# A two-layer diffusion block: modulation by bursts on TensorE, and the remaining row steps in one chain through the up and down passes

## The chip, the cores and the metric

The kernel runs on one core of a Trainium2 chip. The metric is the time of one execution on the device in microseconds (us), given as the median over several runs. A core has engines that run side by side and wait for each other by semaphores: TensorE (PE, matrix multiplications, with its weight loads PEld), VectorE (DVE, elementwise work and reductions), ScalarE (ACT), GpSimd (POOL) and SyncE (SP, which here issues nearly all DMA transfers). Each engine works through its own instructions in a fixed order.

## The reference

Two layers over 1024 latent tokens and 256 context tokens of width 1024. In each layer half of the heads are a bidirectional mLSTM and half a two-dimensional neighbourhood attention; an output projection and a squared-ReLU MLP (1024 to 4096 to 1024) follow. Six modulation vectors of 1024 values (shift, scale and gate for either half of the layer) come from the conditioning vector `c` for the latent tokens and from `c_ctx` for the context:

```python
for l in range(DEPTH):
    need_ctx = l < DEPTH - 1
    mod = silu_c @ w_ada[l] + b_ada[l]          # 1024 -> 6 * 1024
    mod_c = silu_cc @ w_ada[l] + b_ada[l]
    sh1, sc1, g1, sh2, sc2, g2 = split(mod, 6)  # and sh1c ... from mod_c
    h = rmsnorm(x, norm1_g[l]) * (1.0 + sc1) + sh1
    hc = rmsnorm(xc, norm1_g[l]) * (1.0 + sc1c) + sh1c
    y, yc = token_mixers(h @ w_in[l], hc @ w_in[l], ...)   # mLSTM and attention
    x = x + g1 * (y @ w_out[l])
    h = rmsnorm(x, norm2_g[l]) * (1.0 + sc2) + sh2
    x = x + g2 * sq_relu_mlp(h, w_mlp1[l], w_mlp2[l])
    if need_ctx:
        ...                                     # the same for xc with sh1c ... g2c
return rmsnorm(x, final_g)
```

The change is about how `mod` and `mod_c` are computed, a product of two vectors with a 1024 x 6144 matrix per layer, and about where in the program that happens.

## The kernel before

All matrix products are in float32 precision by splitting each operand into a high and a low part and adding three products; the three matmuls of `mm3` are lines L85, L86 and L87, and the splitting of weights is at L80 and L926. The 6144 columns of the modulation are counted as 12 blocks of 512: blocks 0 to 3 are shift and scale of the first half, 4 and 5 the gate `g1`, 6 to 9 shift and scale of the second half, 10 and 11 the gate `g2`.

The first layer's stages in time: an opening to some 70 us, in which blocks 0 to 3 are made; keys, values and gates of the mLSTM to 132 us; the mLSTM output in 20 tiles (`mlstm_out`, `mlstm_tile`) to 449; the neighbourhood attention (`na`, 4 pairs of heads with 2 context blocks and 8 blocks of latent rows each, 40 in all) to 723; the output projection to 840; the up pass of the MLP (`up`) to 1197; the passage to the down pass; the down pass (`down`) to 1505, and a context part to 1625. The second layer follows with the same stages, without context outputs (its attention has 32 blocks) and without any modulation work, since its vectors are made in the first layer.

There are two ways to compute modulation. `ada` does it on TensorE: for each of eight contraction blocks of 128, one matmul per block of 512 columns, with the two silu vectors as 32 stationary columns (L144), each block in its own 32-column tile of the array and its own 32 partitions of one PSUM bank; then a copy of the bank by VectorE (L154), four transposes (L157) and additions of the bias. `ada_rows` does it on VectorE: for each group of 128 output values and each of the two vectors it loads 512 KB of the transposed matrix (L178, tile `wada`, one buffer, with the silu vector as its second half from L175), and one custom instruction multiplies by the silu row and sums (L183, followed by a read of the accumulator). The text calls this a row step. Blocks 4 and 5 are 16 row steps (two vectors), blocks 6 to 9 are 32.

Both are generators. Other code calls `next` on them, so that one piece is issued at a time between other work; the order of each engine is the order in which the code issues. In the first layer's mixers `self.fill` is a chain of row steps for blocks 4 to 9, 48 in all. `tick` takes one piece; it is called at the end of `project_j` (a projection inside the mLSTM output) and after every block of the attention, and whatever is left is issued after the third pair. In `up`, a second chain makes blocks 10 and 11 and the second layer's blocks 0 to 3 (48 steps), three per round with the rest at the last round but one; a third one makes the second layer's blocks 4 to 11 for one vector (32 steps) from round n = 7 of `down` on, every second round, and in the context part.

Other lines that the text names: L475, L495, L601, L611, L612, L624 and L654 are small matmuls and transposes of an mLSTM tile, L493 and L642 DVE work of it; in the attention L823 and L833 are scores, L828 and L834 the maxima on DVE, L839 and L840 the reciprocal and the scaling of the softmax, L848, L859 and L867 transposes, L860 and L868 the copies of them, L874 the product with the values, and L721, L706 and L760 evictions of query, key and output; at the passage L1056 and L1050 store hidden values, L1193 and L1241 load weights and hidden values of the down pass, L1399 loads x, L925 and L926 split what was loaded.

Of the kernel before, what the change touches and what calls it, by code (L numbers as in the profile page):

```python
# [10 lines left out]
F32 = mybir.dt.float32  # L11
# [35 lines left out]
class Kern:  # L47
    def __init__(self, tc, d):
        self.tc, self.nc, self.d = tc, tc.nc, d
        self.fill = iter(())  # L50
# [7 lines left out]
    def tick(self):  # L58

        next(self.fill, None)  # L60
# [72 lines left out]
    def ada(self, l, blocks, tag, pool, bufs):  # L133

        nc, d, ws, nb = self.nc, self.d, [], len(blocks)
# [4 lines left out]
        for k in range(KT + bufs):  # L140
            if k >= bufs:
                w = ws.pop(0)
                for j in range(nb):
                    nc.tensor.matmul(acc[32 * j:32 * j + 32, :], self.silu[:, k - bufs, :], w[:, j, :], start=k == bufs, stop=k - bufs == KT - 1,  # L144
                                     skip_group_check=True, tile_position=(0, 32 * j))
            if k < KT:
                w = pool.tile([128, nb, 512], F32, name="wada", bufs=bufs)
                src = d["w_ada"][l, k * 128:(k + 1) * 128, :].rearrange("p (b c) -> p b c", c=512)
                nc.sync.dma_start(w[:], src[:, blocks[0]:blocks[-1] + 1:blocks[1] - blocks[0], :])
                ws.append(w)  # L150
            yield
        m = 32 * nb
        rv = pool.tile([128, 512], F32, name="arow")
        nc.vector.tensor_copy(rv[:m, :], acc[:m, :])  # L154
        tp = self.bank(tag)
        for t in range(4):
            nc.tensor.transpose(tp[:, t * m:(t + 1) * m], rv[:m, t * 128:(t + 1) * 128], self.ident[:m, :m])  # L157
        for j, b in enumerate(blocks):
            src = tp[:, :4 * m].rearrange("p (t c) -> p t c", t=4)[:, :, 32 * j:32 * j + 2]
            fs = slice(4 * b, 4 * b + 4)  # L160
            nc.vector.tensor_add(mod[:, fs, :], src, self.bada[l][:, fs].unsqueeze(2).to_broadcast([128, 4, 2]))
            for v in range(2):
                self.gain(l, b, v)
        yield

    def ada_rows(self, l, blocks, vectors):
# [5 lines left out]
        t = self.cp.tile([128, 2, D], F32, name="wada")  # L172
        raw, row = t[:, 0], t[:, 1]
# [202 lines left out]
    def project2(self, W, i, hi, lo, tag="mm"):  # L376
        acc = self.bank(tag)
        for u in range(2):
            for k in range(KT):
                wh, wl = W[k // 4]  # L380
                ws = slice((k % 4) * 256, (k % 4) * 256 + 256)
                self.mm3(acc[:, u * 256:(u + 1) * 256], self.toktile(hi[k], 2 * i + u), self.toktile(lo[k], 2 * i + u), wh[:, ws], wl[:, ws], k == 0, k == KT - 1)
        return acc[:].rearrange("p (u c) -> p u c", u=2)

    def project_g(self, W, i, hi, lo, tag="mm", accs=None, ks=range(KT), us=range(2)):

        accs = accs or [self.bank(tag) for _ in range(2)]
        for u in us:
            acc = accs[u]
            for k in ks:  # L390
                wh, wl = W[k // 3]
                ws = slice((k % 3) * 288, (k % 3) * 288 + 288)
                self.mm3(acc[:, :288], self.toktile(hi[k], 2 * i + u), self.toktile(lo[k], 2 * i + u), wh[:, ws], wl[:, ws], k == 0, k == KT - 1)
        return accs

    def project_j(self, W, i, hi, lo, cols):
# [9 lines left out]
        self.tick()  # L406
# [161 lines left out]
    def mlstm_tile(self, l, pr, i, acc):  # L568
# [35 lines left out]
        yield  # L604
        hh = mp.tile([128, 2, 2, 2, 65], F32, name="hh", bufs=1)
# [186 lines left out]
    def na(self, l, hi, lo, need_ctx, Wq, accs, last):  # L792

        self.wide = 1
# [188 lines left out]
    def up(self, l, ctx, B, hi, lo, hp_, hid, filler, last):  # L983
# [155 lines left out]
        def run(pool):  # L1139
            rest_.append(pool)  # L1140
            for j in range(NP):
# [30 lines left out]
    def down(self, l, hid, we, alloc):  # L1172
# [113 lines left out]
        def run(x, mod, load, after, filler):  # L1286
# [3 lines left out]
            for n, (p, b, s) in enumerate(whole):  # L1290
# [10 lines left out]
                if n > 6 and n % 2:  # L1301
                    next(filler, None)
# [236 lines left out]
    def run(self):  # L1539
        nc, d = self.nc, self.d  # L1540
        PS = bass.MemoryType.PSUM
        with self.open(name="pad", side="right") as pad, self.open(name="const") as self.cp, self.open(name="w") as self.wp, \
# [17 lines left out]
            for l in range(DEPTH):  # L1560
# [5 lines left out]
                ada = [chain(self.ada_rows(l, range(10, 12), range(2)), self.ada_rows(l + 1, range(4), range(2))), self.ada_rows(l + 1, range(4, 12), range(1))] if need_ctx else [iter(())] * 2  # L1566
# [16 lines left out]
                with self.open(name=f"x{l + 1}", side="right") as xp, self.open(name=f"up{l}") as hp_, contextlib.ExitStack() as right:  # L1583
# [6 lines left out]
                    prep, lead, rest = self.up(l, need_ctx, B, hi, lo, hp_, hid, ada[0], start)  # L1590
# [53 lines left out]
                with self.open(name=f"xd{l}") as xp, self.open(name=f"sd{l}") as self.sp, self.open(name=f"we{l}") as wx:  # L1644
# [7 lines left out]
                    if l == DEPTH - 1:  # L1652
                        finish(x, mod, load, lambda *a: self.final(x, *a), ada[1])
# [24 lines left out]
                    finish(x, mod, load, after, ada[1])  # L1678
                    run_all(ada[1])
# [150 lines left out]
```

## Time and profile before

| | us |
|---|---|
| median of 3 runs | 2924.03 |
| lowest and highest | 2919.05 and 2924.76 |
| the profiled execution | 2928.78 |
| its span, first to last instruction | 2927.0 |

The mean granted clock of TensorE was 0.991 of full speed in the profiled execution. All durations below are from that execution. In the rows that follow, a group line gives line, engine, operation, tiles (out<-in), shapes and count, then busy us and the mean ns of one, then the idle time ahead of it and what ended it. A line of waits names engine, bank and line that waited, what it waited for, the total us, how often, and the longest. A line of the timeline gives start, duration and, in brackets, the idle time before it. In a line of the chain of work stand start, duration and what the time was spent on. After the change the line numbers are larger by some 5 to 22.

### The profile page before, as it was taken

Reading aid. Unit: us, or ns where it says so; the run is one execution under the profiler, and the core shown is the slowest. Engines: PE = TensorE matmul, PEld = TensorE weight load, DVE = VectorE, ACT = ScalarE, POOL = GpSimd, SP = SyncE. Lnnn points to the kernel's source line nnn. Section 1 sums busy time; section 2 is a strip of 40 time slices with the busy share of each in tenths; the row PEclk is TensorE's granted clock in tenths of the full one; section 3 lists DMA queues with packets and bytes.
Section 4 is the critical chain, followed back from the end, with each engine's and each line's share of the span. In section 5 each row is a group of like instructions: output and inputs, shape, how many; then the busy total and the mean of one; then the engine's idle time right before and its main releaser. Section 6 shows DMA issues by size and latency. Waiting matters only on the chain.

```text
span 2927.0 us, 45550 instructions
## 1 busy us (share of the span) xinstructions
PE 2849.7 (97%) x16512; PEld 2413.8 (82%) x16512; DVE 2252.4 (77%) x5156; ACT 1267.3 (43%) x2426; POOL 67.3 (2%) x117
## 2 busy tenths in 40 slices
PE   7999999998999999999999999999999999999998
PEld 4888888777888888878889988888888788888888
DVE  6789987886598777779878678877875987768774
ACT  5333334454463333344445323335564633334453
POOL 0000000001000000000000000000010000000000
PEclk9999999998999999999999999999999999999999
DMA  7323333555637555797977122213356354469673
GB/s 244 105 94 111 102 99 122 170 186 166 195 113 250 194 191 198 236 366 267 334 266 272 61 87 66 68 62 110 97 154 214 118 183 155 158 233 314 209 254 105
DMA packets 275394, 506.85 MB, mean 173 GB/s; under 512 B 23616, under 2 KB 111680, under 8 KB 275168
## 3 DMA queue, kind: packets, MB, share of 16 engines
q1 hardware_dynamic: 275168, 503.93, 52.2%
q8 instruction: 130, 2.13, 0.3%
q14 instruction: 96, 0.79, 0.1%
HBM read 408.25 MB, written 95.59 MB: 172 GB/s over the span
## 4 chain that ended last, share of the span: by engine, by line
PE 56%; DMA 5%; DVE 5%; ACT 2%; issue 1%; SPq 1%; POOL 0%; DVEq 0%; ACTq 0%; POOLq 0%
PE q L87 11%; PE q L86 11%; PE q L85 11%; PE mm L85 6%; PE mm L86 6%; PE mm L87 6%; PE q L874 1%; PE q L624 1%; DMA wraw<-yscr 1%; DMA wraw<-w_out 1%; DMA raw<-w 1%; DMA wraw<-hid 1%; PE q L848 1%; DVE wlo L80 1%; PE q L833 1%
## 5 line engine op out<-in xcount | busy, mean ns | idle before, releaser
L85 PE MATMUL q<-ah,whi 128*128 128x512 f32 (+1 forms) x1488 | 555.9, 374 | 7.8 <-ACT ah L925 7.3
L86 PE MATMUL q<-al,whi 128*128 128x512 f32 (+1 forms) x1488 | 555.2, 373 | 0.1
L87 PE MATMUL q<-ah,wlo 128*128 128x512 f32 (+1 forms) x1488 | 554.0, 372 | 1.0 <-DVE wlo L926 0.9
L85 PE MATMUL mm<-ah,whi 128*128 128x512 f32 (+1 forms) x1104 | 381.8, 346 | 7.0 <-DVE nq L721 6.2
L87 PE MATMUL mm<-ah,wlo 128*128 128x512 f32 (+1 forms) x1104 | 380.5, 345 | 0.0
L86 PE MATMUL mm<-al,whi 128*128 128x512 f32 (+1 forms) x1104 | 380.4, 345 | 0.0
L85 PEld LDWEIGHTS q<-ah,whi 128*128 128x128 f32 x1488 | 280.8, 189 | 57.9 <-ACT ah L925 8.2
L87 PEld LDWEIGHTS q<-ah,wlo 128*128 128x128 f32 x1488 | 280.8, 189 | 51.4 <-DVE wlo L926 1.8
L86 PEld LDWEIGHTS q<-al,whi 128*128 128x128 f32 x1488 | 281.0, 189 | 50.4 <-issue 1.7
L85 PE MATMUL mm<-whi,ah 128*128 128x512 f32 (+2 forms) x864 | 315.3, 365 | 1.0 <-DVE st L294 0.9
L86 PE MATMUL mm<-wlo,ah 128*128 128x512 f32 (+2 forms) x864 | 311.0, 360 | 0.0
L87 PE MATMUL mm<-whi,al 128*128 128x512 f32 (+2 forms) x864 | 309.6, 358 | 0.0
L85 PEld LDWEIGHTS mm<-ah,whi 128*128 128x128 f32 x1104 | 209.6, 190 | 33.3 <-DVE nq L721 6.8
L87 PEld LDWEIGHTS mm<-ah,wlo 128*128 128x128 f32 x1104 | 209.7, 190 | 25.5 <-issue 0.7
L86 PEld LDWEIGHTS mm<-al,whi 128*128 128x128 f32 x1104 | 209.8, 190 | 24.4 <-issue 0.2
L925 ACT CAST ah<-raw 128x512 fp32r<-128x512 f32 (+1 forms) x264 | 144.1, 566 | 141.5 <-PE q L87 69.3
L85 PEld LDWEIGHTS mm<-whi,ah 128*128 128x128 f32 x864 | 164.6, 191 | 25.4 <-PE q L475 1.3
L87 PEld LDWEIGHTS mm<-whi,al 128*128 128x128 f32 x864 | 164.8, 191 | 23.2 <-issue 0.5
L86 PEld LDWEIGHTS mm<-wlo,ah 128*128 128x128 f32 x864 | 165.0, 191 | 22.0 <-issue 0.5
L926 DVE TENSOR_TENSOR al<-raw,ah 128x512 fp32r<-128x512 f32 (+1 forms) x264 | 158.1, 620 | 27.7 <-ACT ah L925 27.5
L183 DVE CUSTOM_DVE_ANT_0 wada<-wada,consts 128x1024 f32<-128x1024 f32 x128 | 163.3, 1276 | 19.9 <-DMA wada<-w_adaT 19.6
L926 DVE TENSOR_TENSOR wlo<-raw,whi 128x1024 fp32r<-128x1024 f32 x84 | 102.4, 1222 | 77.3 <-ACT whi L925 74.9
(278 smaller groups left out, 5292.0 us busy)
## 6 DMA issues: line engine op xcount, KB each, us to landing
raw<-w SPq DMA_DIRECT2D x168, 512.0 KB
wada<-w_adaT SPq DMA_DIRECT2D x128, 512.0 KB
raw<-hid SPq DMA_DIRECT2D x104, 512.0 KB
wraw<-w SPq DMA_DIRECT2D x80, 512.0 KB
hid<-hb SPq DMA_DIRECT2D x128, 256.0 KB
hid<-ht SPq DMA_DIRECT2D x96, 256.0 KB
gb<-gscr SPq DMA_DIRECT2D x36, 512.0 KB
wraw<-w_j SPq DMA_DIRECT2D x32, 512.0 KB
```

The costliest lines, as they stand in the source:

```text
L80: nc.vector.tensor_sub(lo[:, :n], raw[:, :n], fview(hi[:, :n]))
L85: mm(out, lh, rh, start=start, stop=False, skip_group_check=True)
L86: mm(out, lh, rl, start=False, stop=False, skip_group_check=True)
L87: mm(out, ll, rh, start=False, stop=stop, skip_group_check=True)
L183: nc.vector.tensor_tensor_reduce(raw, raw, row, 1.0, self.bada[l][:, i:i + 1], ALU.mult, ALU.add, mod[:, i, v:v + 1])
L624: nc.tensor.matmul(n4[:, s, h, :], P[:, s, h, :], va[:, u, h, :], start=True, stop=True, skip_group_check=True)
L833: mm(sl[:, :nl].rearrange("p (r w) -> p r w", w=Rw[1]), q[2 * h + z], krhs[h], start=z == 0, stop=z == 1)
L848: nc.tensor.transpose(tp[:, (h * 2 + a) * 128:(h * 2 + a + 1) * 128], Pn[h][:, a * 128:(a + 1) * 128], self.ident)
L874: mm(yp[h * 64:(h + 1) * 64, :], v[h], pt[h], start=i == 0, stop=i == len(tiles) - 1, skip_group_check=True)
L925: ins = self.nc.scalar.copy(hi, src)
L926: self.nc.vector.tensor_sub(lo, src, fview(hi))
```

## The change

Blocks 6 to 9 of the first layer move from row steps to `ada` on TensorE. `ada` gets a second form for `bufs=1`: four blocks share one tile of weights, so a column slice is 256 instead of 512 wide, two contraction blocks are loaded together (two DMAs of 512 KB), and one burst of eight matmuls (L150) works through them. Two column slices of four such bursts make eight bursts. The pieces are taken at more places: `project2` and `project_g`, which belong to keys, values and gates, as well as `project_j` and each `mlstm_tile`. Blocks 4 and 5 stay row steps, but in a second generator, `self.rows`, of which `tick(True)` takes a piece only when `fill` is used up. The attention no longer ticks; `na` issues what is left of both at its start. In `up` and `down`, one chain holds all 80 row steps: three per round of `up` to the fourteenth round and one in the last two, then every second round of `down` from n = 3 on, and then in the context part.

```diff
-    def tick(self):
-
-        next(self.fill, None)
+    def tick(self, rows=False):
+
+        if next(self.fill, self) is self and rows:
+            next(self.rows, None)
...
-    def ada(self, l, blocks, tag, pool, bufs):
+    def ada(self, l, blocks, tag, pool=None, bufs=1):
...
+        n = 1024 // nb
+        todo = [(k, o) for o in range(0, 512, n) for k in range(KT)]
+        two = 2 if bufs == 1 else 1
+        def through(k, o, w):
+            for z in range(two):
                 for j in range(nb):
-                    nc.tensor.matmul(acc[32 * j:32 * j + 32, :], self.silu[:, k - bufs, :], w[:, j, :], ...)
+                    nc.tensor.matmul(acc[32 * j:32 * j + 32, o:o + n], self.silu[:, k + z, :], w[:, z, j, :], ...)
+        for i in range(0, len(todo) + bufs * two, two):
+            if i >= bufs * two:
+                through(*todo[i - bufs * two], ws.pop(0))
+            if i < len(todo):
+                k, o = todo[i]
+                w = pool.tile([128, two, nb, n], F32, name="wada", bufs=bufs)
+                for z in range(two):
+                    src = d["w_ada"][l, (k + z) * 128:(k + z + 1) * 128, :].rearrange("p (b c) -> p b c", c=512)
+                    nc.sync.dma_start(w[:, z], src[:, blocks[0]:blocks[-1] + 1:blocks[1] - blocks[0], o:o + n])
+                    if z < two - 1:
+                        yield
                 ws.append(w)
             yield
...
     def project2, project_g (at their ends)
+        self.tick()
...
     def project_j
-        self.tick()
+        self.tick(True)
...
     def mlstm_tile (after the copy of qT)
+        self.tick(i in (2, 4))
...
     def na
+        run_all(self.fill)
+        run_all(self.rows)
...
-                self.tick()
             run_all(nxt)
-            if pr == 2:
-                run_all(self.fill)
...
     def up
-                for _ in range(2):
+                for _ in range(2 if j < NP - 2 else 0):
                     next(filler, None)
-                if j == NP - 2:
-                    run_all(filler)
...
     def down
-                if n > 6 and n % 2:
+                if n > 2 and n % 2:
                     next(filler, None)
...
     def mixers
-            self.fill = chain(*(self.ada_rows(l, blocks, range(2)) for blocks in (range(4, 6), range(6, 10))))
+            self.fill = self.ada(l, range(6, 10), "q")
+            self.rows = self.ada_rows(l, range(4, 6), range(2))
...
-                ada = [chain(self.ada_rows(l, range(10, 12), range(2)), self.ada_rows(l + 1, range(4), range(2))), self.ada_rows(l + 1, range(4, 12), range(1))] if need_ctx else [iter(())] * 2
+                ada = chain(*(self.ada_rows(*a) for a in ((l, range(10, 12), range(2)), (l + 1, range(4), range(2)), (l + 1, range(4, 12), range(1))) if need_ctx))
```

What this does to the order of the engines is shown at three places. The first is PE in one of the mLSTM output tiles; `mm<-whi,ah` are the projections' matmuls, `q<-kva,P` the product with the values. Before:

```order
L624 MATMUL q<-kva,P 128x65 x8
L85 MATMUL mm<-whi,ah_89 128x512
L86 MATMUL mm<-wlo,ah_89 128x512
L87 MATMUL mm<-whi,al_113 128x512
L85 MATMUL mm<-whi,ah_92 128x512
L86 MATMUL mm<-wlo,ah_92 128x512
```

Now:

```order
L646 MATMUL q<-kva,P 128x65 x8
L150 MATMUL q<-wada,silu 32x256 x8
L86 MATMUL mm<-whi,ah_89 128x512
L87 MATMUL mm<-wlo,ah_89 128x512
L88 MATMUL mm<-whi,al_113 128x512
L86 MATMUL mm<-whi,ah_92 128x512
```

A burst of eight matmuls stands behind the product with the values and ahead of the next projection; the fourth to the eighth burst lie so, one in each of five tiles.

The second place is DVE in the attention's first pair. `nq` and `nk1` are the query and key evictions, `S` the scores of a block, `smax` and `ssum` their maximum and sum. Before:

```order
L721 TENSOR_TENSOR nq_5133<-mm_5102,nq_5133 64x512
L721 TENSOR_TENSOR nq_5134<-mm_5102,nq_5133 64x512
L706 SCALAR_TENSOR_TENSOR nk1_5160<-mm_5169,nk1_5160 64x256
L183 ISA wada_4396,mod_179<-wada_4396,consts_153 128x1024
L183 ISA mod_179 128x1
L839 RECIPROCAL ssum_5208<-ssum_5208 128x1
L828 ISA S_5212,smax_5213<-q_5200,zero_159 128x256
```

Now:

```order
L743 TENSOR_TENSOR nq_5231<-mm_5200,nq_5231 64x512
L743 TENSOR_TENSOR nq_5232<-mm_5200,nq_5231 64x512
L728 SCALAR_TENSOR_TENSOR nk1_5258<-mm_5267,nk1_5258 64x256
L860 RECIPROCAL ssum_5304<-ssum_5304 128x1
L849 ISA S_5308,smax_5309<-q_5296,zero_159 128x256
```

The row step between the evictions and the softmax of the next block is gone, as are all 30 in this stage; the rest of DVE's order is as it was.

The third place is SP at the passage from up to down, from the first load of hidden values to the loads of x (`hid` and `hidc0` are stores of hidden values, `wraw<-w2` and `raw<-w2` the down weights). Before:

```order
L178 DMA wada_10647<-w_adaT 128x1024
L1193 DMA wraw_12727<-w2 128x2x512
L178 DMA wada_10647<-w_adaT 128x1024
L1056 DMA hid0_81<-hb_12683 128x512
L1241 DMA wraw_12733<-hid0_81 128x2x512
L1056 DMA hid0_81<-ht_12719 128x512
L1193 DMA wraw_12791<-w2 128x2x512
L178 DMA wada_10647<-w_adaT 128x1024
L1056 DMA hid0_81<-hb_12716 128x512
```

Now:

```order
L1212 DMA wraw_12747<-w2 128x2x512
L1077 DMA hid0_81<-hb_12701 128x512
L1260 DMA wraw_12753<-hid0_81 128x2x512
L196 DMA wada_10680<-w_adaT 128x1024
L1077 DMA hid0_81<-ht_12739 128x512
L1077 DMA hid0_81<-hb_12736 128x512
L1077 DMA hid0_81<-ht_12740 128x512
L1071 DMA hidc0_82<-hx_12807 128x256
L1212 DMA wraw_12811<-w2 128x2x512
```

Between the first load of hidden values and the loads of x there were six row loads, and now there is one; two more stand later, between the down weights, at n = 3 and n = 5.

More of the change, by code (lines that the diff above doesn't have):

```diff
@@ L139, in ada @@
         acc = self.bank(tag)
-        for k in range(KT + bufs):
-            if k >= bufs:
-                w = ws.pop(0)
+        n = 1024 // nb
[3 more added lines that the diff above has]
+            for z in range(two):
                 for j in range(nb):
-                    nc.tensor.matmul(acc[32 * j:32 * j + 32, :], self.silu[:, k - bufs, :], w[:, j, :], start=k == bufs, stop=k - bufs == KT - 1,
+                    nc.tensor.matmul(acc[32 * j:32 * j + 32, o:o + n], self.silu[:, k + z, :], w[:, z, j, :], start=k + z == 0, stop=k + z == KT - 1,
                                      skip_group_check=True, tile_position=(0, 32 * j))
[L146 to L149, printed above, removed]
+        for i in range(0, len(todo) + bufs * two, two):
[9 more added lines that the diff above has]
+                        yield
                 ws.append(w)
             yield
-        m = 32 * nb
-        rv = pool.tile([128, 512], F32, name="arow")
-        nc.vector.tensor_copy(rv[:m, :], acc[:m, :])
+        m = 32 * len(blocks)
+        if bufs == 1:
+            row = pool.tile([128, two, nb, n], F32, name="wada")
+            rv = row[:].rearrange("p z b c -> p (z b c)")
+        else:
+            rv = pool.tile([128, 512], F32, name="arow")
+        nc.vector.tensor_copy(rv[:m, :512], acc[:m, :])
         tp = self.bank(tag)
@@ L171, in ada_rows @@
         mod = self.mod
-        t = self.cp.tile([128, 2, D], F32, name="wada")
-        raw, row = t[:, 0], t[:, 1]
+        t = self.cp.tile([128, 2, 4, 256], F32, name="wada")
+        raw, row = t[:, 0].rearrange("p b c -> p (b c)"), t[:, 1].rearrange("p b c -> p (b c)")
         for v in vectors:
@@ L1652, in run @@
                     if l == DEPTH - 1:
[L1653 removed]
+                        finish(x, mod, load, lambda *a: self.final(x, *a), ada)
                         continue
@@ L1676, in after @@
                             nc.sync.dma_start(xscr[z * 512:(z + 1) * 512, g0:g0 + n].rearrange("(a p) t -> p a t", p=128), x[gi][z][:])
-                    finish(x, mod, load, after, ada[1])
-                    run_all(ada[1])
+                    finish(x, mod, load, after, ada)
+                    run_all(ada)
                     hi, lo = nact
```

9 lines of the change are left out of this document (6 added, 3 removed).

## The prediction

> **What bounds the kernel now.** I read the page's first part, then busy time by stage, then TensorE's waits in the stages that the change touches, then single instructions. The page says that TensorE (PE) is nearly full and VectorE (DVE) comes next:
>
> ```profile
> span 2927.0 us, 45550 instructions
> PE 2849.7 (97%) x16512; PEld 2413.8 (82%) x16512; DVE 2252.4 (77%) x5156; ACT 1267.3 (43%) x2426; POOL 67.3 (2%) x117
> ```
>
> So a microsecond of PE idle or of half clock is what a change can win, and work put on PE costs its full length wherever PE is full. Busy time by stage (columns: stretch, its length, then per engine busy us and instructions; granted clock, DMA share, GB/s) shows where either holds:
>
> ```profile
> 132.00:449.00 317.00, 316.30 (x1898) 264.71 (x1897) 273.06 (x1038) 108.17 (x286) 16.38 (x35) 1.00 0.32 101
> 449.00:665.00 216.00, 201.76 (x1492) 170.59 (x1491) 184.79 (x525) 114.40 (x258) 5.15 (x7) 0.98 0.51 162
> 665.00:723.00 58.00, 50.27 (x453) 44.28 (x452) 39.16 (x145) 31.04 (x77) 8.99 (x7) 0.88 0.51 153
> ...
> 1197.00:1270.00 73.00, 66.90 (x320) 56.02 (x319) 43.24 (x62) 24.50 (x38) 0.00 (x0) 0.95 0.87 304
> 1270.00:1505.00 235.00, 235.00 (x1036) 194.20 (x1035) 209.04 (x312) 111.91 (x178) 0.00 (x0) 1.00 0.88 308
> 1996.00:2224.00 228.00, 223.56 (x1722) 189.92 (x1721) 176.34 (x523) 127.03 (x270) 9.22 (x7) 1.00 0.40 122
> 2564.00:2640.00 76.00, 74.64 (x330) 61.37 (x329) 45.37 (x61) 28.09 (x41) 0.00 (x0) 1.00 0.72 252
> ```
>
> 132 to 449 is the first layer's mLSTM output (20 tiles): PE idles 0.7 us in 317. 449 to 723 is its neighbourhood attention, in which the row steps end at 665; 1996 to 2224 is the same stage of the second layer, which has no row steps. 1197 to 1270 is the passage from up to down pass in the first layer, 2564 to 2640 the one in the second. The attention and the passage are where the first layer is worse than the second: 14.24 us idle (216.00−201.76) at clock 0.98 and 7.73 idle at 0.88, against 4.44 idle at full clock.
>
> Who PE waits for in the attention (first fence 449 to 665, second 665 to 723, third the second layer; total, times, longest):
>
> ```profile
> PE mm L85 <- DVE nq L721: 6.2, 3, 3.2
> PE q L848 <- DVE S L840: 5.2, 6, 1.3
> PE q L833 <- DVE nyT L760: 1.1, 1, 1.1
> ```
> ```profile
> PE q L874 <- ACT pl L868: 4.0, 3, 2.7
> PE q L874 <- DVE smax L834: 1.9, 1, 1.9
> ```
> ```profile
> PE q L874 <- ACT pl L868: 2.3, 4, 1.0
> ```
>
> While row steps run, PE waits for DVE: for the eviction of a query projection (L721) and for the softmax scaling (L840). In the second layer it waits for neither. Such a wait also costs clock:
>
> ```profile
> 527.75 0.80 PE L85 MATMUL mm<-ah,whi 128*128 128x512 f32 x1 [3.20 <-DVE nq L721]
> 528.35 0.63 PE L86 MATMUL mm<-al,whi 128*128 128x512 f32 x1
> ...
> 531.25 0.39 PE L85 MATMUL mm<-ah,whi 128*128 128x512 f32 x1
> ```
>
> After 3.20 us of waiting, the same form takes 0.63 to 0.80 us instead of 0.39, for some 3.4 us.
>
> **The change part by part.**
>
> *Row steps leave the attention.* Its 30 steps are on DVE, each a reduction and the read of its accumulator (82 ns median):
>
> ```profile
> L183 DVE CUSTOM_DVE_ANT_0 wada<-wada,consts 128x1024 f32<-128x1024 f32 x30 | 38.3, 1276 | 7.0 <-DMA wada<-w_adaT 6.8
> ...
> L183 DVE DVE_READ_ACCUMULATOR2_ANT mod<- x128: 73/82/88, 134.1 to 1597.5; 128x1 f32 x128
> ```
>
> 30 × 1.358 = 40.7 us of DVE go, which leaves 184.8−40.7 = 144 of some 200 us (72%) for the blocks before 665, under the second layer's 176.3 of 228 (77%). With them go 30 loads of 512 KB on SP, which nothing here was shown to wait for. The loss is idle plus clock: 14.24 + 0.02 × 216 = 18.6 us to 665 and 7.73 + 0.12 × 58 = 14.7 after it, 33.3 in all. The second layer's 4.44 over 32 blocks, scaled to the 40 blocks here, is 5.3. The upper end of the gain is thus 28.0; the lower end cures only the stretch that holds steps, 18.6 − 5.3 × 216/274 = 14.4. The stretch after 665 holds no step, but the blocks in it are begun before, so its waits are partly lateness carried over: I take half of the 13.6 between the ends, a gain of 21 (14.4 + 6.8 = 21.2).
> [...]
>
> *Eight bursts on PE.* The opening already has such matmuls, two 32-column tiles per contraction block, between 128x288 matmuls that start 0.13 us apart:
>
> ```profile
> 41.96 1.91 PE L144 MATMUL mm<-wada,silu 128*32 128x512 f32 x8
> 43.80 0.40 PE L85 MATMUL q<-whi,ah 128*128 128x288 f32 x1
> ...
> 45.10 0.29 PE L85 MATMUL q<-whi,ah 128*128 128x288 f32 x1
> 45.23 0.29 PE L86 MATMUL q<-wlo,ah 128*128 128x288 f32 x1
> 45.36 0.30 PE L87 MATMUL q<-whi,al 128*128 128x288 f32 x1
> 45.59 1.05 PE L144 MATMUL mm<-wada,silu 128*32 128x512 f32 x4
> 46.57 0.40 PE L85 MATMUL q<-whi,ah 128*128 128x288 f32 x1
> ```
>
> Two matmuls of 512 columns (four records, x4) put the next matmul off by 46.57−45.36−0.13 = 1.08 us, 0.98 of it from their start. Now a burst is eight matmuls of 256 columns in four 32-column tiles, so if four tiles stream side by side, it has the same column time: 2 contraction blocks × 256 columns × 2 passes. If only two do, it is twice that, 1.84 (43.80−41.96) and a head of 0.10. The records of x4 start in pairs, and only two tiles stood in line there, so the row shows no limit at two; since two tiles on separate columns share their time, I take four. No trace of before shows four. Burst one is split in two halves (0.23 more); the third lies before a wait in the value projections and is covered; the rest have no cover, because the tiles idle 0.7 us in 317:
>
> ```profile
> PE q L495 <- DVE vw L493: 2.4, 1, 2.4
> ```
> ```profile
> PE q L495 <- DVE bs L642: 0.7, 3, 0.2
> ```
>
> Four transposes come at the end, by the row of four in the second layer's attention 0.49 us, with the change of form 0.6:
>
> ```profile
> 2060.60 0.66 PE L848 MATMUL q<-consts,S 128*128 128x128 f32 x4
> 2061.09 0.60 PE L859 MATMUL q<-consts,S 128*96 128x128 f32 x4
> ```
>
> 7 × 1.08 + 0.23 + 0.6 = 8.4 us on the path; the ends are 5 (two more bursts fall into waits) and 7 × 1.94 + 0.23 + 0.6 = 14.4 (two tiles at a time).
> [...]
>
> DVE's new work, one copy of the bank (0.68 us for the opening's smaller copy, by the same 512 columns) and four adds, replaces 32 steps. The bank that is held from the value projections to the eighth burst leaves five of six to the tiles: 0 to 1.4 us (seven tiles at the longest wait above, 0.2), taken as 0. Each chunk is two loads of 512 KB, and SP issues them only when the burst before is through; behind them on SP stand the tile's gate load and output store. DMA is at 0.32 in that stage and a tile lasts 317/20 = 15.9 us, which hides both.
>
> *The row steps that stay in the mixers.* 16 instead of 18 in the tiles, two in some tiles. Without steps a tile has (273.06 − 18 × 1.36)/20 = 12.4 us of DVE, with two 15.1 of 15.9: cost 0, about 1 us a tile if DVE's order makes a tile late.
>
> *Up, down and context.* 48 steps become 44 in up, 32 become 36 behind it. PE is full in down (235.00 of 235) with DVE at 89%, so 4 × 1.36 us more DVE there (and in the context part) cost 0; without the cover, 5.4.
>
> *The passage to down.* PE's longest wait and the chain of work that leads to it:
>
> ```profile
> PE q L85 <- ACT ah L925: 6.0, 1, 6.0
> ```
> ```profile
> PE q L85 <- ACT ah L925: 1.4, 1, 1.4
> ```
> ```profile
> 1211.72 5.10 DMA wada<-w_adaT
> 1216.84 1.28 DVE wada L183
> 1218.17 3.16 DMA wada<-w_adaT
> ...
> 1236.84 0.44 SPq L178
> ...
> 1249.21 12.98 DMA raw<-w
> ```
>
> The first is this passage, the second that of the second layer, which has no steps. SP had six row loads between its first load of the hidden rows and the loads of x; now one. The queue runs at some 390 GB/s from 1240 on, so 512 KB are 1.3 us, and two row loads with a step lie on the chain itself (9.5 us). The loss is 6.0 + 0.05 × 73 = 9.7 against 1.4: the gain ends at 8. But two steps (n = 3 and 5) now put loads between the down pass's own behind the x loads, 2 × 1.3 = 2.6 of delay if the weights run late. Ends −8 and +3; I take −5, 8.3 less 2.6 rounded, since the second layer's passage is the nearest row.
>
> **Sum.** −21 + 8.4 + 0 + 0 − 5 = −17.6 us. The profiled execution took 2928.78 us (span 2927.0), 4.75 above the median of the runs, 2924.03; I put the change on the median: 2906.4, say 2907.
>
> **The rivals.** What a measurement of this kernel can tell from no change is 0.2%, 5.8 us: faster is below 2918.2, slower above 2929.9.
>
> *B, all losses heal.* The stretch after 665 becomes like the second layer's, and the passage too, with two more bursts covered: −28 + 5 − 8 = −31, 2893. For it speaks that DVE's share falls below the second layer's; against it that ACT, not DVE, releases the longest waits after 665.
>
> *C, the bursts eat the gain.* Two tiles at a time (+14.4), only the stretch with steps cured (−14.4), passage unchanged: 2924, no change. For it: more than two tiles is nowhere shown, and after 665 there are no steps to remove.
>
> *D, slower: a burst waits for its chunk.* Bursts 4 to 8 stand in PE's in-order queue one per tile, and all of the tile's matmuls stand behind them. A chunk is issued only after the burst before, waits on SP behind the gate load and travels in 1 KB pieces. If each lands 4 us late, the wait is 4 and the half clock after it costs about 1.7 (half of 3.4 us, from the row at 527.75): 5 × 5.7 = 28.5. With nothing else changed in the sum, 2907 + 28.5 = 2935. The point from which it ends slower is a mean lateness of about 3 us, a chunk that needs some 19 us from the burst before it; against it, the rows show 512 KB in 3.2 to 5.1 us, so two take about 10 of the 15.9.
>
> That the change does not do what it says can be left out: in the order of the changed kernel no row step stands in the attention.
>
> **How the numbers follow.** Forecast 0.59 (its own range 2899 to 2917), B 0.13, C 0.17, D 0.08, and 0.03 for small effects that cancel. The likeliest gives 2907. The range 2894 to 2924 leaves out the lower half of B, the upper half of C and D, about 0.2. Faster: forecast less a little of its upper edge, and B, 0.72. Same: C, that edge and the small effects, 0.19. Slower: D and a part of C's upper half, 0.09.
>
> **What the profile after would show.** PE idle in the first layer's attention of some 10 us instead of 22 and a clock near 1.00 up to its last pair, with no wait for L721's or L840's successors above 2 us; if waits on DVE stay there, the steps were not their cause. Bursts of about 1.0 us from start to next matmul; 1.9 would be C. No wait of a burst for its weights above 0.3 us; several above 3 would be D. PE's wait at the start of down near 2 us; 6 or more would show the x loads themselves as its cause. The forecast fails if the tail of the attention keeps its clock of 0.88 and the bursts take two tiles at a time.

## The result, and the profile after

The change took 2897.42 us (median of 4 runs, 2896.26 to 2898.96) against 2924.4 (4 runs): a ratio of 0.9912, 95% interval 0.9895 to 0.9929. That is 27.0 us less, where 17 were forecast: inside the range (2894 to 2924), but a little below the forecast's own one (2899 to 2917). The first lines of the page after:

```profile
span 2897.0 us, 45725 instructions
PE 2839.9 (98%) x16644; PEld 2405.4 (83%) x16644; DVE 2217.4 (77%) x5097; ACT 1264.8 (44%) x2426; POOL 67.2 (2%) x117
```

DVE's share is the same; PE idles less. Since both kernels do the same 4000 triples of L85 to L87 (now L86 to L88), the start of the n-th of them in each trace says how far ahead or behind the kernel is at that place. The steps in it: +6.6 us up to 240 us (the bursts; 0.1 of it stands before 70), nothing in the remaining tiles, −29.6 in the attention, −1.1 in the output projection, nothing through the up pass, −6.4 at the passage to down, +0.6 behind it. Nothing else moved: −29.9 for two profiled executions that are 29.8 apart (2928.78 and 2898.96).

Busy time of the attention alone, from the first score of its first pair to its last product, first before, then after; PE does the same 1874 instructions in both:

```profile
462.00:722.70 260.70, 238.73 (x1874) 203.63 (x1874) 214.93 (x655) 138.53 (x319) 14.13 (x14) 0.96 0.52 163
```
```profile
468.60:699.70 231.10, 224.76 (x1874) 195.82 (x1874) 180.79 (x590) 137.88 (x319) 14.14 (x14) 1.00 0.36 109
```

Idle goes from 22.0 to 6.3 us, and the same instructions are busy for 14.0 us less. The clock, 1.00 in place of 0.96, accounts for some 10 of these. What PE still waits for there, all of it short:

```profile
PE q L895 <- ACT pl L889: 2.9, 3, 2.0
PE q L869 <- DVE S L861: 1.1, 1, 1.1
```

A burst in an mLSTM tile (16 records), and the passage and its wait:

```profile
155.67 0.39 PE L646 MATMUL q<-kva,P 128*128 128x65 f32 x2
155.98 1.07 PE L150 MATMUL q<-wada,silu 128*32 128x256 f32 x16
156.98 0.50 PE L86 MATMUL mm<-whi,ah 128*128 128x512 f32 x1
```
```profile
1172.90:1239.50 66.60, 64.91 (x320) 54.74 (x319) 34.18 (x46) 24.16 (x37) 0.00 (x0) 1.00 0.82 287
```
```profile
PE q L86 <- ACT ah L946: 1.7, 1, 1.7
```

The burst takes 1.00 us to the next matmul, so four tiles stream side by side: the starts of four records lie within 0.02 us in the trace, and the next four follow 0.22 to 0.24 us later. No burst waited for its weights.

### The profile page after: what moved, and what is told of

Its sections match the earlier page's. It is cut to its first block, busy times and chain, and to the rows that moved or that the text cites. A ratio compares the mean times of both kernels' runs of the same rounds, so it can differ in the third digit from the quotient of the medians.

```text
span 2897.0 us, 45725 instructions
## 1 busy us (share of the span) xinstructions
PE 2839.9 (98%) x16644; PEld 2405.4 (83%) x16644; DVE 2217.4 (77%) x5097; ACT 1264.8 (44%) x2426; POOL 67.2 (2%) x117
## 5 line engine op out<-in xcount | busy, mean ns | idle before, releaser
L86 PE MATMUL q<-ah,whi 128*128 128x512 f32 (+1 forms) x1488 | 555.1, 373 | 3.3 <-ACT ah L946 2.2
L88 PE MATMUL q<-ah,wlo 128*128 128x512 f32 (+1 forms) x1488 | 553.4, 372 | 1.2 <-DVE wlo L947 1.1
L87 PE MATMUL q<-al,whi 128*128 128x512 f32 (+1 forms) x1488 | 553.9, 372 | 0.0
L86 PE MATMUL mm<-ah,whi 128*128 128x512 f32 (+1 forms) x1104 | 380.0, 344 | 2.1 <-ACT ah L905 2.0
L88 PE MATMUL mm<-ah,wlo 128*128 128x512 f32 (+1 forms) x1104 | 379.0, 343 | 0.5 <-DVE wlo L81 0.5
L87 PE MATMUL mm<-al,whi 128*128 128x512 f32 (+1 forms) x1104 | 379.0, 343 | 0.0
L86 PEld LDWEIGHTS q<-ah,whi 128*128 128x128 f32 x1488 | 280.3, 188 | 53.8 <-ACT ah L946 3.0
L88 PEld LDWEIGHTS q<-ah,wlo 128*128 128x128 f32 x1488 | 280.3, 188 | 51.3 <-DVE wlo L947 2.3
L87 PEld LDWEIGHTS q<-al,whi 128*128 128x128 f32 x1488 | 280.4, 188 | 49.4 <-issue 1.4
L86 PE MATMUL mm<-whi,ah 128*128 128x512 f32 (+2 forms) x864 | 314.0, 364 | 0.6 <-DVE st L312 0.4
L87 PE MATMUL mm<-wlo,ah 128*128 128x512 f32 (+2 forms) x864 | 310.0, 360 | 0.0
L88 PE MATMUL mm<-whi,al 128*128 128x512 f32 (+2 forms) x864 | 309.1, 358 | 0.0
L86 PEld LDWEIGHTS mm<-ah,whi 128*128 128x128 f32 x1104 | 209.0, 189 | 28.3 <-ACT ah L905 2.6
L88 PEld LDWEIGHTS mm<-ah,wlo 128*128 128x128 f32 x1104 | 209.1, 189 | 25.3 <-DVE wlo L81 1.0
L87 PEld LDWEIGHTS mm<-al,whi 128*128 128x128 f32 x1104 | 209.1, 189 | 24.1
L86 PEld LDWEIGHTS mm<-whi,ah 128*128 128x128 f32 x864 | 164.2, 190 | 27.5 <-issue 3.2
L88 PEld LDWEIGHTS mm<-whi,al 128*128 128x128 f32 x864 | 164.4, 190 | 23.2 <-issue 0.9
L87 PEld LDWEIGHTS mm<-wlo,ah 128*128 128x128 f32 x864 | 164.6, 190 | 21.9 <-issue 0.2
L86 PE MATMUL q<-th,whi 128*128 128x512 f32 x384 | 150.1, 391 | 2.5 <-DVE s L1111 2.3
```

What stands on the lines that cost most here:

```text
L86: mm(out, lh, rh, start=start, stop=False, skip_group_check=True)
L87: mm(out, lh, rl, start=False, stop=False, skip_group_check=True)
L88: mm(out, ll, rh, start=False, stop=stop, skip_group_check=True)
```

## Experiments

All ratios are to the kernel before in the same batch of runs; "over the change" is the difference of medians to 2897.4. Where a profile is read, it is that of one execution, and executions of the kernels with steps in the attention spread over up to 12 us. The kernel before has medians of 2924.4 to 2926.7 us in the batches, so 2 us of a difference of medians can be chance.

| run | median us | ratio, 95% interval |
|---|---|---|
| the change | 2897.4 | 0.9912 (0.9895 to 0.9929) |
| mixers' part alone | 2903.3 | 0.9919 (0.9906 to 0.9931) |
| chain part alone | 2919.4 | 0.9976 (0.9966 to 0.9986) |
| + 29 reductions in the attention | 2913.7 | 0.9949 (0.9932 to 0.9966) |
| + 30 loads there | 2901.4 | 0.9911 (0.9897 to 0.9924) |
| + 29 complete steps there | 2924.6 | 0.9999 (0.9990 to 1.0008) |
| the same, two buffers | 2922.0 | 0.9983 (0.9973 to 0.9993) |
| order of before, no steps | 2910.8 | 0.9957 (0.9943 to 0.9972) |
| complete steps, order of the change | 2929.6 | 1.0012 (1.0002 to 1.0021) |
| reductions, order of the change | 2916.2 | 0.9973 (0.9964 to 0.9983) |
| + loads at the passage | 2905.9 | 0.9930 (0.9916 to 0.9943) |
| all 48 steps in the mixers, no bursts | 2917.7 | 0.9974 (0.9963 to 0.9984) |
| half on TensorE | 2917.6 | 0.9974 (0.9965 to 0.9983) |

**The two parts apart.** The first run takes the change but leaves `up` and `down` as they were:

```diff
-                ada = chain(*(...))
+                ada = [chain(self.ada_rows(l, range(10, 12), range(2)), self.ada_rows(l + 1, range(4), range(2))), self.ada_rows(l + 1, range(4, 12), range(1))] if need_ctx else [iter(())] * 2
...
-                for _ in range(2 if j < NP - 2 else 0):
+                for _ in range(2):
                     next(filler, None)
+                if j == NP - 2:
+                    run_all(filler)
...
-                if n > 2 and n % 2:
+                if n > 6 and n % 2:
```

> The mixers' part alone: blocks 6 to 9 by bursts, no steps in the attention, up and down as before. If the parts add up, it keeps the bursts (+6.6) and the attention (-29.6) and gives back the passage (6.4): some 23 us under before, 2901, and some 6 above the whole change, with PE's wait at the start of down at 6 us again. Rival, the passage was cured because the up pass starts earlier or with another order of SP: then it stays cured, 2895 to 2898, and the wait is under 2 us.

The second makes the same edit the other way round on the kernel before.

> The chain through up and down alone, the mixers as before. If the parts add up: 6 to 7 us under before, 2918, all of it at the passage, with the attention's 22 us of idle and its half clock unchanged. Rival (the two loads put at n = 3 and 5 cost, and only the whole change hides them): no gain or a loss, 2924 to 2928.

2903.3 and 2919.4, so 23.4 and 7.3 us under before: the sum, 30.6, lies within the interval of the change (20.8 to 30.7), and the place shows it better. In the first the wait at the start of down is back, in the second it is gone while the attention is 260.0 us long, as before:

```profile
PE q L86 <- ACT ah L946: 6.0, 1, 6.0
```
```profile
PE q L85 <- ACT ah L925: 2.0, 1, 2.0
```

The two loads at n = 3 and 5 cost nothing that either trace shows.

**What made the passage wait.** Each of the two steps at the end of `up` loads its 512 KB four times; one reduction each, as in the change:

```diff
-                    nc.sync.dma_start(raw, d["w_adaT"][l, i])
+                    for _ in range(1 + self.more):      # more = 3 at j >= NP - 2 of the first layer
+                        nc.sync.dma_start(raw, d["w_adaT"][l, i])
```

> The whole change, but each of the two row steps at the end of the up pass loads its 512 KB four times, so that five row loads instead of one stand on SP between the first load of hidden values and the loads of x; DVE does no more than in the change. If the loads were the cause at the passage: PE's wait at the start of down goes from 1.7 to 5 or 6 us and the time to 2902 to 2904. Rival, DVE's reductions there were the cause: within 2 us of the change.

The wait came back, longer than it was before, with five row loads in place of six:

```profile
PE q L87 <- ACT ah L948: 7.1, 1, 7.1
```

The trace falls 7.2 us behind that of the change between 1200 and 1260 us, and at no other place by more than 2. So the loads ahead of the down weights were enough for the whole of it, and the reductions weren't needed. (2905.9 is some 2 us above the range expected; 1.8 of this execution's lag stand before the passage.)

**What made the attention wait.** Into the change went, after each block of the first three pairs: reductions on a resident tile of zeros; then loads without a reader; then both, as `ada_rows` has them.

```diff
+        extra = self.extra(30) if l == 0 else iter(())
...
+                if pr < 3:
+                    next(extra, None)      # a load of w_adaT[0, i], and one block later its reduction
```

> The whole change, but 29 row steps without their loads put into the attention's first three pairs (the reduction runs on a resident tile of zeros). If DVE's time was the cause of the waits there, the attention gets slower by about what was won, 25 to 30 us, 2922 to 2927, and its last pair loses clock again. Rival, the loads on SP and the DMA queues were the cause: within 3 us of the change, 2897 to 2900.

> The whole change, but the 30 loads of 512 KB put into the attention's first three pairs, without reductions and with no reader. If DVE's time was the cause: within 3 us of the change, 2897 to 2900. Rival, the loads: 10 to 30 us slower, 2907 to 2927, with PE waiting for blocks whose bias tables or values come late.

> The whole change, with 29 complete row steps (a load of 512 KB into one buffer, then the reduction that waits for it) put back into the attention; their sums go to an unused place. Reductions alone cost some 16 to 18 us and loads alone 2 to 4. If DVE's wait for a load that is not there in time is the missing part (its 30 steps waited 7.0 us before), the attention is back where it was, 28 to 30 us slower than in the change: 2924 to 2927. Rival, the parts only add up: 18 to 22 slower, 2916 to 2920.

16.3, 4.0 and 27.1 us over the change: the reductions cost less than was expected, the loads a little more, and the complete steps what was expected. The 4.0 of the loads are hardly told from nothing: their ratio, 0.9911, is that of the change, and the attention is 1.8 us longer in the trace. Complete steps bring all of the loss back, so it was the steps and nothing else in the mixers' part; the sum of the two halves is 7 short. In the profiles the attention (in the same stretch as above) takes 249.4 us with reductions, 232.9 with loads, 261.6 with both, against 231.1:

```profile
468.20:717.60 249.40, 236.71 (x1876) 199.03 (x1874) 212.54 (x649) 137.66 (x318) 14.17 (x14) 0.99 0.36 107
```
```profile
468.90:701.80 232.90, 225.64 (x1876) 195.81 (x1874) 180.85 (x591) 137.90 (x319) 14.24 (x14) 1.00 0.49 151
```
```profile
467.40:729.00 261.60, 238.61 (x1876) 201.28 (x1874) 213.93 (x648) 138.89 (x319) 14.42 (x14) 0.97 0.51 160
```

With reductions (the slowest of four executions, 2918.9), 6.4 of the 18.3 us that the stage lasts longer are idle time of PE. The other 12.0 are busy time of the same instructions, and two stretches of 3.4 us at half clock (granted clock 0.99 over the stage) make only 3.4 of them: so the larger part is neither a wait nor the clock.

DVE is just as busy with complete steps as with reductions (213.9 and 212.5 us), yet the stage is 12 us longer. One thing that differs is in DVE's own rows: the idle time ahead of the reduction, with complete steps and then with two buffers, the next run, in which each load is issued one block earlier:

```profile
L216 DVE CUSTOM_DVE_ANT_0 wada<-wada,consts 128x1024 f32<-128x1024 f32 x29 | 37.1, 1280 | 10.3 <-DMA wada<-w_adaT 10.1
```
```profile
L217 DVE CUSTOM_DVE_ANT_0 wada<-wada,consts 128x1024 f32<-128x1024 f32 x29 | 36.9, 1273 | 0.1
```

> As the run before it, but with two buffers, so that each load is issued one block earlier than its reduction. If waiting for loads is the missing part: about the reductions and loads alone, 18 to 22 us over the change, 2915 to 2920. Rival, the missing part lies in the order of TensorE's work: as the run before it, 2924 to 2927.

2922.0: neither. DVE no longer stands before a step that has no data, and the attention is shorter in the profile (254.6 against 261.6), but the medians are 2.6 us apart with executions from 2915 to 2927. That DVE waits for loads has a part of some microseconds. The loads still add something (24.6 over the change, where reductions and loads alone make 20.3), and one wait of this trace shows how they can: DVE stands 3.7 us for the bias table of a block (`S<-rpbt`), a load of the kernel's own, and PE then waits 5.9 us for DVE's scaling of a softmax, the longest of the four waits in the second line. With reductions alone DVE waits 0.7 us for such tables.

```profile
DVE S L872 <- DMA S<-rpbt: 3.7, 1, 3.7
```
```profile
PE q L886 <- DVE S L878: 8.6, 4, 5.9
```

How much of the 24.6 goes this way stays open.

**The order of TensorE's work.** The traces showed something the prediction had not looked at. In the second half of the first pair of the first layer's attention, PE has 48 matmuls of the next pair's projections between the blocks. After the change they stand in five pieces, 38 of them in the last two; before it, they are scattered in ten pieces of 1 to 14 and begin two blocks earlier, and with reductions put back it is much the same. This order is not the code's, which is the same for these matmuls in all of these kernels: it is made when the kernel is built, and steps on DVE change it. (That the order of each engine is the order in which the code issues, as said of the kernel before, thus does not hold here; nor is the rest of DVE's order in the attention as it was, as said of the change: there, too, the two traces differ in more than the steps.) The next run takes the change, without steps, and holds PE in the attention to the order of before:

```diff
+            pe = [pe[k] for a, n in ORDER for k in range(a, a + n)]
+            for a, b in zip(pe, pe[1:]):
+                self.tc.add_manual_dep(b, a.name, ...)      # b is issued after a; no wait
```

> The whole change, no steps in the attention, but TensorE's matmuls there are held in the order that they had before (a table of 154 pieces, by edges of order alone). In that order the next pair's projections are taken up early, one to five at a time, and few are left for the pair's end. If the reductions and loads themselves were the cause: within 3 us of the change, 2897 to 2900. Rival, the order that they lead the scheduler to is the missing part: 8 to 12 us over it, 2905 to 2910.

13.4 us over the change, with DVE about as free as in the change (183.75 us busy, 180.79 there). The attention and PE's longest wait in it, in the slowest of the four executions (2917.4):

```profile
469.20:715.50 246.30, 232.54 (x1876) 200.34 (x1874) 183.75 (x591) 138.37 (x318) 14.19 (x14) 0.98 0.34 104
```
```profile
PE mm L89 <- DVE nq L746: 7.5, 3, 3.1
```

This is the wait that the prediction quoted from before as its first sign of a late DVE (L721, 6.2 us, three times, 3.2 at most), at the same three places, one for each pair to come, and there is no step on DVE. In that order PE has used up most of the projections when it comes to the pair's end; by the names, the next one (bank mm) waits until DVE has evicted a query projection (nq). So that wait comes with the order alone, without the steps.

Is the order then the missing part? The steps again, with PE held to the order of the change:

> 29 complete row steps in the attention as in the run that took 2924.6, but TensorE's matmuls held in the order of the change. If the order has no part: 2922 to 2927 again. Rival, the order has a part of 8 to 12 us: 2913 to 2917.

> 29 reductions without loads as in the run that took 2913.7, with TensorE's matmuls held in the order of the change. If the order has no part: 2912 to 2916. Rival: 2903 to 2907, since what is left is DVE's time alone.

2929.6 and 2916.2, 5.0 and 2.5 us more than with the order that the scheduler chose for these kernels, with 95% intervals that overlap a little in either pair. With steps, the order of the change is thus no better, and PE's waits only change their place: in the scheduler's order the complete steps had two on the query eviction (3.4 us) and six on the softmax scaling (6.3), now there are twelve on the scaling, the other row that the prediction had quoted.

```profile
PE q L897 <- DVE S L889: 14.2, 12, 3.1
```

So the order is no separate part that could be added to the steps. The order of before costs 13 us where DVE is not late; where it is, the order of the change is no better than the scheduler's. What the two trade can be seen with reductions, here in the order of the change:

```profile
467.20:718.90 251.70, 232.59 (x1875) 200.01 (x1874) 212.68 (x649) 138.28 (x319) 14.18 (x14) 0.98 0.34 104
```

PE is idle for 19.1 us and busy for 232.6; in the scheduler's order it was idle for 12.7 and busy for 236.7, at a slightly better clock (0.99 against 0.98). Scattered projections fill waits, but PE is busy longer with the same instructions; why it is, no run here shows. The steps themselves cost 16 (reductions) to 27 us (complete) in the scheduler's order.

**Was TensorE needed?** All 48 steps for blocks 4 to 9 on DVE, in the mixers ahead of the attention; then half of them, with blocks 8 and 9 in four bursts on TensorE:

```diff
-            self.fill = self.ada(l, range(6, 10), "q")
-            self.rows = self.ada_rows(l, range(4, 6), range(2))
+            self.rows = self.ada_rows(l, range(4, 10), range(2))        # first run
+            self.fill = self.ada(l, range(8, 10), "q")                  # second run
+            self.rows = self.ada_rows(l, range(4, 8), range(2))
...
-        self.tick(i in (2, 4))
+        self.tick(True)        # first run: in project2 and project_g as well
```

> No bursts: all 48 steps for blocks 4 to 9 as row steps on DVE, up to 47 of them in keys, values, gates and the 20 mLSTM tiles, none in the attention; up and down as in the change. DVE would be busy for about 12.4 + 2 x 1.36 = 15.1 us of each tile's 15.9. If that fits: 6 us under the change, 2891. Rival, DVE has too little room so near to full and PE waits for it: each of 32 more steps costs up to 1.36 us, up to 40 us over the change; I expect some 10 us over it, 2900 to 2915.

> Half of the move: blocks 8 and 9 by four bursts of eight records pairs on TensorE, blocks 4 to 7 as 32 row steps in the mLSTM tiles (about 1.5 a tile), none in the attention. TensorE has 4 x 1.1 = 4.4 us less to do than in the change, DVE 16 x 1.36 = 21.8 more, 14.5 of a tile's 16. If the tiles hold that: 2893 to 2895, under the change. Rival, as with all 48 steps there: PE waits for DVE, half of the 20 us lost there minus what TensorE saves, 2901 to 2906.

2917.7 and 2917.6, 20 us over the change, both of them, though one has 32 more steps on DVE and the other 16. So it is not the sum of DVE's time alone: in both, the trace falls behind that of the change at the same two places, by 10 us in either run between 270 and 310, and by 7 and 5 between 360 and 390 (the first run also loses 5.6 near 115 and wins most of it back by 240, where the change has its bursts). Either place is a change of pairs, the second and the third of three, where the next pair's weights have to be split on DVE (wlo, L81) and PE waits for that (first all 48 steps, then half):

```profile
PE mm L87 <- DVE wlo L81: 5.2, 2, 3.1
```
```profile
PE mm L87 <- DVE wlo L81: 4.6, 2, 2.6
```

In the second run a row step stands just ahead of the split:

```profile
295.52 1.27 DVE L201 CUSTOM_DVE_ANT_0 wada<-wada,consts 128x1024 f32<-128x1024 f32 x1
...
297.92 1.22 DVE L81 TENSOR_TENSOR wlo<-wraw,whi 128x1024 fp32r<-128x1024 f32 x1
```

The split is not all of it. PE waits for DVE twice more at this place, for a rotary product (ropeb) and for weighted scores (P), and works at half clock from these two waits on, some 7 us ahead of the wait for the split, until 303.4:

```profile
PE mm L87 <- DVE wlo L81: 2.1, 1, 2.1
PE mm L86 <- DVE ropeb L439: 1.3, 1, 1.3
PE q L646 <- DVE P L644: 1.0, 1, 1.0
```
```profile
280.00:289.80 9.80, 7.46 (x40) 6.26 (x39) 9.16 (x33) 5.15 (x12) 0.96 (x2) 1.00 0.47 161
289.80:303.40 13.60, 11.52 (x53) 8.56 (x52) 11.44 (x42) 2.54 (x8) 0.00 (x0) 0.50 0.39 134
```

That is 4.4 us of waits and 6.8 of lost clock. The first run has 4.3 and 6.8 at this place; at the other the two have 3.5 and 3.0 us of waits and 3.4 and 1.7 of lost clock. The granted clock was 0.91 in both from 240 to 320 us, and 0.93 and 0.97 from 360 to 410.

The kernel of the change gives out two steps a tile only at i = 2 and 4, away from a pair's first tile. A version with half on TensorE and no extra step near a change of pairs might do better than the change; it was not run.

## Why the prediction was right, and where a size was off

*The bursts.* Right: four tiles at a time, 1.00 us from a burst's start to the next matmul (0.98 by the row of before), and rival C's 1.9 did not come. In all they cost 6.6 us where 8.4 were taken, and the difference is luck. By 110 us, with two bursts done, the trace is 2.1 us behind; at 132, with three done, only 0.3. Before the change the value projections' wait of 2.4 us was followed by half clock, 1.7 us lost; after it they wait 1.9 us in two pieces, and the clock stays:

```profile
128.40:131.80 3.40, 3.40 (x10) 2.66 (x9) 3.40 (x19) 0.00 (x0) 0.00 (x0) 0.50 0.72 235
```
```profile
120.00:132.00 12.00, 10.08 (x97) 7.97 (x96) 7.82 (x26) 4.14 (x9) 0.00 (x0) 1.00 0.98 329
```

Without that the bursts cost 8.3.

*Rival D.* No burst waited for its chunk at all.

*The passage.* −6.4 us for −5 (8.3 less 2.6 gives 5.7, which the sum took as 5). The wait went from 6.0 to 1.7 and the half clock behind it with it (granted clock 0.95 in the stage before, 1.00 after), and the run with loads alone shows the cause as the prediction had it: row loads on SP and the queues ahead of the first down weights.

*The attention.* This is the term that was mis-sized: −21 taken, −29.6 measured, beyond the upper end of 28.0. Two steps of the working failed. The first is the half that was taken of the stretch behind the steps. Counted as the prediction counted, by idle time and clock, the last pair (from its first score on) lost 14.7 us before, 7.7 of them idle, and loses 3.5 after, all of them idle: 11.1 won of the 13.6 that could be had, where 6.8 were taken. What carries the loss into that pair, in which no block has a step, is not settled: it lost 10.3 with the chain part alone, where the attention is as before, 8.3 with complete steps put back, and 5.4 with the order of before and no steps. Before the change the granted clock was 0.88 from 665 us on; after it, it is 1.00 in the last pair. The first three pairs were sized well by the same count: 17.5 us lost before, 2.8 after, 14.7 won where 14.4 were taken. The second step is a term that the working does not have. It counts idle time and clock alone, but PE's busy time for the same instructions shrank by 14.0 us, and the clock accounts for 10.2 (20.5 us at half clock before, none after). The other 3.7 came with another order of PE's work; their cause is not shown. (By length the first three pairs went from 202.0 to 180.0 us and the last from 58.7 to 51.2, but after the change 17 instructions that had stood in the first three stand in the last.) The 5.3 us that the working leaves to this stage is 4.44 scaled by time; by blocks, as its text says, it would be 5.6, which lowers both ends by 0.2 to 0.3.

*The reading of the waits* was half right. That the steps cause the loss is shown: put back complete, they cost it all. That PE waits "for DVE" at L721 was read as DVE being late. The run with the order of before and no steps has the same wait. And DVE's time was taken for all of the cause: reductions alone cost 16.3 of the 27.1 us, and the loads, "which nothing here was shown to wait for", matter together with them: DVE's row in the prediction itself had 6.8 us of waiting for them, and it was not used.

*The steps that stayed in the mixers, and up and down*, cost nothing, as predicted: the trace does not move between 240 and 449 us nor in the up pass. The runs with more steps in the mixers show the edge of that: an average of DVE's time per tile (14.5 to 15.1 of 15.9 us) said that they would fit, and they did not, at two changes of pairs where PE waits for DVE and its clock goes (0.50 in the stretch of 13.6 us above).

B's 2893 was nearer to the measured time than the forecast's 2907, by its −28 for the attention; that its 5 for the bursts is near the measured 6.6 is the luck told above. It was given 0.13, and the evidence that was set against it (ACT releases the longest waits of the last pair) did not decide: ACT still releases the longest one there, 2.0 us after and 2.7 before, but now no half clock follows it (granted clock 1.00 from 648.5 to 699.7 us).

## What to carry to other kernels

A wait's releaser is the last thing that came, not the cause: whether an engine is late, or the waiting engine was sent there too early by its order, is told by holding the order and taking the load away, or the other way round: here the order of before alone brought 7.5 us of waits for the query evictions, with no step on DVE. Work on a second engine that runs full of short dependent steps can cost the first engine much of its duration, here 27 us of PE for 29 steps that fill DVE for 39, part of it through the loads that it waits for in its own queue; ask for the stage where the first engine has a stream of independent work instead, and keep it clear of the few places where that stage too has a deadline. And the chain at a passage between stages is worth looking through for transfers that nobody needs there.

## What the runs showed of the hardware

In the change, 16 records of 256 columns on four 32-column tiles of the array took 1.07 us; in the opening of before, 4 records of 512 columns on two tiles took 1.05. That is twice the columns in the same time.

A wait of 2.0 us was followed by half clock in one trace and not in the other. At the start of the second layer's up pass PE waits 1.99 us in the trace of before and 2.01 us in that of after. Behind the wait the matmuls take 0.63 us in the first and 0.39 in the second:

```profile
2329.31 0.50 PE L85 MATMUL q<-th,whi 128*128 128x512 f32 x1 [1.99 <-DVE s L1090]
...
2330.22 0.63 PE L85 MATMUL q<-th,whi 128*128 128x512 f32 x1
```
```profile
2300.04 0.50 PE L86 MATMUL q<-th,whi 128*128 128x512 f32 x1 [2.01 <-DVE s L1111]
...
2300.84 0.39 PE L86 MATMUL q<-th,whi 128*128 128x512 f32 x1
```

The granted clock was 0.50 from 2330.0 to 2333.4 us in the first, with 0.99 in the 3.5 us ahead of it and 1.00 in the 3.4 us behind it; in the second it was 1.00 from 2297.0 to 2307.2. Two waits do not show what sets them apart.

Executions of the kernel with two buffers, in which PE idles 15.4 us in the attention against 6.3 in the change, spread over 12 us (2915 to 2927), and those of the change over 3. Whether the clock has a part in that is not shown either.
